# A decoder step on one core: weight forms of the first MLP pair earlier, squares loaded by another queue, last weights kept

## The chip, the core and the metric

The kernel runs on one core of a Trainium2 chip. The core has five engines with a queue of instructions each: TensorE (PE in the profile) multiplies, VectorE (DVE) and ScalarE (ACT) work element by element, GpSimd (POOL) does a little of that and issues DMAs, SyncE (SP) only issues DMAs. Each engine takes its instructions in order; semaphores order the engines among each other. SBUF is the memory that the engines work from, PSUM the memory that TensorE writes to, and DRAM is reached by DMA.

The metric is the time of one execution on the device, in microseconds (us), and of several runs the median.

## What is computed

One layer of a decoder for a prompt of 1024 tokens and 8 samples of 8 tokens, 1088 columns in all, width 1024, all in float32. Four token mixers share one input projection; their outputs are projected, gated, summed and projected again. Then comes the part that the change touches:

```python
x = x + g1 * out                                        # out = (gated sum of the branches) @ w_out
h2 = rmsnorm(x, p["norm_mlp_g"][l]) * (1.0 + sc2) + sh2
x = x + g2 * (jnp.square(jax.nn.relu(h2 @ p["w_mlp1"][l])) @ p["w_mlp2"][l])
...
y = rmsnorm(x, p["norm_final_g"])
```

w_mlp1 is 1024 x 4096, w_mlp2 4096 x 1024.

## The kernel before

**Layout and products.** Activations lie with the features on 128 partitions and the 1088 columns along the free axis: eight tiles for the width, 32 for the hidden layer. A float32 product is made of three products of a rounded format: each operand is split into a high part (a rounded copy, ACT) and a low part (what is left, DVE), by `split`, and hi x hi, lo x hi and hi x lo are summed in PSUM. A weight block of 512 x 128 is loaded to a staging tile `wst` by SP's queue and split to `whi` and `wlo` (`weights`). There are three buffers of `wst` and four each of `whi` and `wlo`, so a load waits for a split, and a split for the products that read the old block.

**Order.** Nothing is ordered by hand here: a scheduler orders every engine's instructions by a priority (program order, unless `tc.high_priority(offset=...)` moves a piece ahead by that many instructions) and by a simulated clock. Weight blocks and evacuations of PSUM are moved ahead by `PRIO` = 3000 instructions, the second half's column forms by twice that. The order is fixed when the program is built, and an engine whose next instruction has to wait holds everything behind it.

**Memory.** Pools of SBUF are stacks, one from the left and one from the right end. A pool that is closed gives its place to later pools, and a tile there waits until the instructions that used the overlapping old tiles are done.

**w_out and the columns' forms.** The 1088 columns are two halves (`HALF` = 544) of two quarters (`QU` = 272). For each half, `w_out` is multiplied from the tiles M, the residual is added (`add_resid`) and the squares are summed for the norm (`add_sq`). `norm_terms(c)` and `column_forms(c)` then make, for half c, the norm's factor and seven operands called B11, B21, T1 to T4 and B22: parts of the normalised half and differences of such parts. `column_forms(0)` runs beside the second half's w_out; `column_forms(1)` needs w_out's last sums.

**MLP1** is a product of 2 x 2 blocks made with seven block products instead of eight. `seven_weights` loads the four blocks of two row tiles (a11, a12, a21, a22), makes four sums and differences of them on DVE (s3, s1, s2 and the last one, in place but for s3, which has the tile `wcm`) and splits seven forms, W1 to W7. They are made in the order W1, W2, W5, W6, W7, W4, W3. The first four lie in the pool `wp` that all weights use, the last three in a pool `xw`, which also holds a22 and `wcm`. `xw` is the last pool on the left, above the forms, where w_out's operands M were. `seven` multiplies the forms: pa, pb, pe, pc are its PSUM tiles, each with W1, W2, W5 or W4 first, and W6, W7, W3 added later. There are 16 such pairs of row tiles, `j`; for the first one `seven` runs once for each half, later for both halves at once. Each of the 14 products of a pair is 12 TensorE products. `evac` squares the result, splits it and stores the two parts to DRAM (`asc`, tensors ah and al) by POOL's queue.

**MLP2** takes the 32 hidden tiles in groups (`GROUPS`). The first two stay in SBUF (`KK`); all others are loaded again, as two tiles of 544 KB each, into `NA` = 9 buffers for each part, by SP's queue. For each group and each of the eight row tiles `mt`, `gemm_quarters` multiplies the group's blocks of w2 with the columns and `ev` adds to the residual R. In the second group the residual from before the MLP is loaded (`xr`) and added. The last group runs over three column groups, (0, 1), (2,) and (3,), so that the final norm of one can run beside the next. It loads and splits its eight w2 blocks in each of them. After each column group come the norm's product over the partitions (`rms`), Ln and Exp on ACT, and the multiplication, by ACT and POOL for the first two and part of the last, by DVE for the rest.

## Time and profile before

| | us |
|---|---|
| median of 3 runs | 2477.72 |
| lowest and highest of them | 2475.24, 2478.2 |
| the profiled execution | 2474.55 |
| its span, first to last instruction | 2472.8 |
| TensorE busy within the span | 2394.4 |
| VectorE, ScalarE, GpSimd busy | 1375.8, 1035.5, 306.0 |

The profile is one execution. A page gives each engine's busy time, 40 slices of the span, DMA queues, and the chain of work that ended last. A row of time order reads: start, length, engine, line, operation, output<-inputs, shape, count, and in brackets how long the engine had stood idle and what ended that. A line like L107 is that of a helper (`mm`), so tile names tell more than lines. A row of windows reads: from and to, length, busy time and count, granted TensorE clock (1.00 is full), DMA share, GB/s. The stages that matter here lie so in the span: w_out to 1694 us, MLP1 from there to about 2055, MLP2 to the end.

### The profile page before, as it was taken

To read this page: it belongs to the slowest core of one execution; us is meant where nothing else is said; L and a number is where in the kernel's file an instruction comes from. 1 tells how busy PE (TensorE), PEld (TensorE's weight loads), DVE (VectorE), ACT (ScalarE), POOL (GpSimd) and SP (SyncE) were. 2 spreads that over 40 slices of the span, in tenths; PEclk is the share of its full clock that TensorE was granted. 3 is DMA by queue.
4 is the path that set the end of the run, shared out by engine and by line. 5 is a ranking of instruction groups with operands and counts; after the bars stand their busy time and mean duration, and the time that the engine had idled before them with its cause. 6 is when DMAs were issued, how large, how long until landed. Compare 5 with 4: busy or idle time off the path is not lost.

```text
span 2472.8 us, 46690 instructions
## 1 busy us (share of the span) xinstructions
PE 2394.4 (97%) x19150; PEld 2236.7 (90%) x19150; DVE 1375.8 (56%) x2540; ACT 1035.5 (42%) x1849; POOL 306.0 (12%) x479
## 2 busy tenths in 40 slices
PE   6999999999999999999999999997999999999996
PEld 4998898988998988889888999997999998999996
DVE  6666445746266473656734676768655552422247
ACT  5522545225344234542256553455666663111115
POOL 0102200012101021000111000001222221000003
PEclk9999999999999999999999999999999999999998
DMA  7333221241322232213322464532655657425244
GB/s 258 129 88 95 94 70 63 80 111 57 106 69 70 81 94 91 74 64 85 100 90 107 148 215 164 175 120 89 184 155 154 158 151 266 156 100 189 68 153 135
DMA packets 189140, 300.45 MB, mean 122 GB/s; under 512 B 57320, under 2 KB 105400, under 8 KB 188928
## 3 DMA queue, kind: packets, MB, share of 16 engines
q1 hardware_dynamic: 138512, 217.79, 27.9%
q0 software_dynamic: 47104, 74.44, 9.9%
q10 hardware_dynamic: 3312, 5.25, 0.6%
q8 instruction: 150, 2.46, 0.4%
q14 instruction: 62, 0.51, 0.1%
HBM read 211.29 MB, written 81.66 MB: 118 GB/s over the span
## 4 chain that ended last, share of the span: by engine, by line
PE 83%; DVE 7%; DMA 4%; ACT 3%; issue 2%; SPq 0%; ACTq 0%; DVEq 0%; POOL 0%; POOLq 0%
PE pg L107 57%; PE pa L107 6%; PE pe L107 4%; PE sm L107 2%; PE pc L107 2%; PE pb L107 2%; PE pu L107 2%; DVE X L101 2%; PE ada L107 1%; PE G L107 1%; PE pyr L107 1%; PE po L107 1%; DMA adaw<-ada 1%; DVE wlo L101 1%; DMA g<-gst 1%
## 5 line engine op out<-in xcount | busy, mean ns | idle before, releaser
L107 PE MATMUL pg<-Hh,whi 128*128 128x362 f32 (+1 forms) x1872 | 625.9, 335 | 1.0 <-ACT gst L98 0.7
L107 PE MATMUL pg<-Hh,wlo 128*128 128x362 f32 (+1 forms) x1872 | 626.6, 335 | 0.0
L107 PE MATMUL pg<-Hl,whi 128*128 128x362 f32 (+1 forms) x1872 | 621.0, 334 | 0.0
L98 ACT ACTIVATE whi<-wst 128x512 fp32r<-128x512 f32 (+1 forms) x404 | 250.0, 620 | 609.7 <-PE pg L107 534.8
L101 DVE TENSOR_TENSOR wlo<-wst,whi 128x512 fp32r<-128x512 f32 (+1 forms) x404 | 278.5, 690 | 380.9 <-ACT whi L98 380.1
L107 PEld LDWEIGHTS pg<-Hh,whi 128*128 128x128 f32 x1872 | 352.6, 188 | 12.5 <-issue 2.3
L107 PEld LDWEIGHTS pg<-Hl,whi 128*128 128x128 f32 x1872 | 352.3, 189 | 8.5 <-DVE Hl L104 0.8
L107 PEld LDWEIGHTS pg<-Hh,wlo 128*128 128x128 f32 x1872 | 352.9, 189 | 7.6
L107 PE MATMUL pg<-ah,whi 128*128 128x272 f32 x960 | 276.4, 290 | 2.9 <-ACT whi L98 2.9
L107 PE MATMUL pg<-ah,wlo 128*128 128x272 f32 x960 | 277.3, 290 | 1.4 <-DVE wlo L101 1.4
L107 PE MATMUL pg<-al,whi 128*128 128x272 f32 x960 | 273.8, 290 | 0.0
L107 PEld LDWEIGHTS pg<-ah,whi 128*128 128x128 f32 x960 | 181.9, 190 | 3.5 <-ACT whi L98 3.3
L107 PEld LDWEIGHTS pg<-ah,wlo 128*128 128x128 f32 x960 | 182.1, 190 | 2.2 <-DVE wlo L101 2.0
L107 PEld LDWEIGHTS pg<-al,whi 128*128 128x128 f32 x960 | 180.3, 190 | 0.0
L104 DVE SCALAR_TENSOR_TENSOR cacc<-u,pv,cacc 128x1024 f32<-128x1024 f32 x120 | 153.8, 1281 | 2.1
L104 DVE SCALAR_TENSOR_TENSOR R<-pg,mod,R 128x544 f32<-128x544 f32 (+2 forms) x120 | 65.7, 570 | 136.7 <-PE pg L107 136.7
L107 PE MATMUL pg<-yh,whi 128*128 128x362 f32 (+1 forms) x384 | 127.5, 332 | 1.1 <-DVE gt L101 1.1
L107 PE MATMUL pg<-yh,wlo 128*128 128x362 f32 (+1 forms) x384 | 126.6, 330 | 0.0
L107 PE MATMUL pg<-yl,whi 128*128 128x362 f32 (+1 forms) x384 | 126.2, 329 | 0.0
L1181 POOL DMA_DIRECT2D g<-gst x96 | 53.5, 557 | 390.0 <-ACT gst L98 377.5
L98 ACT ACTIVATE gst<-pg 128x362 f32<-128x362 f32 (+1 forms) x96 | 45.4, 473 | 126.2 <-PE pg L107 111.6
L699 POOL TENSOR_SCALAR sp<-St,dec 128x64 f32<-128x64 f32 x60 | 58.5, 975 | 229.2 <-DVE St L104 208.0
(443 smaller groups left out, 4757.3 us busy)
## 6 DMA issues: line engine op xcount, KB each, us to landing
wst<-w SPq DMA_DIRECT2D x136, 256.0 KB, 3.3
adaw<-ada SPq DMA_DIRECT2D x48, 512.0 KB, 7.2
wst<-w_in SPq DMA_DIRECT2D x92, 256.0 KB, 2.9
gt<-g SPq DMA_DIRECT2D x32, 544.0 KB, 4.1
wst<-w_gate SPq DMA_DIRECT2D x64, 256.0 KB, 2.9
ah<-ah POOLq DMA_DIRECT2D x60, 272.0 KB, 2.7
al<-al POOLq DMA_DIRECT2D x60, 272.0 KB, 4.3
ah<-ah SPq DMA_DIRECT2D x30, 544.0 KB, 9.0
```

The source lines that it names most:

```text
L98: return self.nc.scalar.activation(out, in_, func, bias=bias, scale=scale)
L101: return self.nc.vector.tensor_tensor(out, a, b, op=op)
L104: return self.nc.vector.scalar_tensor_tensor(out, a, s, b, op0=op0, op1=op1)
L107: return self.nc.tensor.matmul(out, lhsT, rhs, start=start, stop=stop, skip_group_check=True)
L699: nc.gpsimd.tensor_scalar(sp, St, dec[:, c:c + 1], None, op0=OP.mult)
L1181: nc.gpsimd.dma_start(d[:, n0:n0 + n], t[:, :n])
```

## The change

It has these parts.

- **First pair's weight forms.** The pool `xw` is on the right now, between the two residual pools, and open before w_out. `seven_weights` for the first pair (`W0`) stands right behind `column_forms(0)` in the program, ahead of `column_forms(1)`. Of the seven forms, the first two and the last two lie in `wp` and the middle three in `xw`.
- **Column forms.** Each form is one tile of four blocks instead of four tiles. `column_forms` works on four blocks with one operation in the first half and on two in the second. The tile `sqt` in w_out is a quarter wide instead of a half.
- **MLP2's loads.** They go by GpSimd's queue. The groups are (0, 1), (2, 3), (4..11), (12..19), (20..27), (28..31); before they were (0, 1), (2..7), (8..15), (16..23), (24..27), (28..31). The loaded tiles lie lowest in their memory, the residual above them; `xr` and `sqt` have a pool of their own.
- **Last group.** Its eight split blocks are kept in a pool `fw` and used for all three column groups. The final norm of a column group stands behind the third row tile of the next one. Its multiplications are done by DVE, except k = 2 and 5 of the last column group, which ACT and POOL do as before.

```diff
-    def weights(self, ap, prio=True):
+    def weights(self, ap, prio=True, pool=None, bufs=WHI):
...
-            hi = self.wp.tile([128, 4, 128], F32R, name="whi", tag="whi", bufs=WHI)
-            lo = self.wp.tile([128, 4, 128], F32R, name="wlo", tag="wlo", bufs=WHI)
+            hi = (pool or self.wp).tile([128, 4, 128], F32R, name="whi", tag="whi", bufs=bufs)
+            lo = (pool or self.wp).tile([128, 4, 128], F32R, name="wlo", tag="wlo", bufs=bufs)
...
-        for j, (ap, ks) in enumerate(parts):
-            hi, lo = self.weights(ap)
+        for j, (W, ks) in enumerate(parts):
+            hi, lo = W if isinstance(W, tuple) else self.weights(W)
...
-                pool = self.wp if next(n) < 4 else self.xw
+                pool = self.wp if next(n) in (0, 1, 5, 6) else self.xw
...
-    pools = right(last, "resb"), right(ractx, "resa")
+    xctx = ExitStack()
+    pools = [right(last, "resb")]
+    net.xw = right(xctx, "xw")
+    pools.append(right(ractx, "resa"))
...
-        part = lambda k, h: R[:, k, h * QU:h * QU + QU]
+
+        step = 2 if c else 4
+        part = lambda k, h: R[:, k:k + step, h * QU:h * QU + QU]
+
+        def split_form(f, i, src):
+            net.split(F[f][0][c][:, i:i + step], F[f][1][c][:, i:i + step], src)
+
         for f, o in (("B11", 0), ("B21", 4)):
-            for i in range(4):
-                normed(i + o)
+            for i in range(0, 4, step):
+                for k in range(i, i + step):
+                    normed(k + o)
                 split_form(f, i, part(i + o, 0))
...
-            for i in range(4):
+            for i in range(0, 4, step):
                 net.tt(part(i + out[0], out[1]), part(i + a[0], a[1]), part(i + b[0], b[1]), OP.subtract)
                 split_form(f, i, part(i + out[0], out[1]))
-        for i in range(4):
+        for i in range(0, 4, step):
             split_form("B22", i, part(i + 4, 1))
...
-                F[f][p][c] = [fpool.tile([128, QU], F32R, name=f"{f}{'hl'[p]}{c}{i}") for i in range(4)]
-    net.xw = left(fctx, "xw")
+                F[f][p][c] = fpool.tile([128, 4, QU], F32R, name=f"{f}{'hl'[p]}{c}")
     column_forms(0)
+    W0 = net.seven_weights((A["w1"][0], A["w1"][1]))
     net.stage.close()
...
-                W = net.seven_weights((A["w1"][2 * j], A["w1"][2 * j + 1]))
+                W = net.seven_weights((A["w1"][2 * j], A["w1"][2 * j + 1])) if j else W0
...
-            rp, ap_ = left(m, "resid"), left(m, "ap")
+            ap_, rp, mp = left(m, "ap"), left(m, "resid"), left(m, "misc")
...
-            GROUPS = ((0, 1), (2, 3, 4, 5, 6, 7), tuple(range(8, 16)), tuple(range(16, 24)), (24, 25, 26, 27), (28, 29, 30, 31))
+            GROUPS = ((0, 1), (2, 3)) + tuple(tuple(range(i, i + 8)) for i in (4, 12, 20)) + ((28, 29, 30, 31),)
...
-                            nc.sync.dma_start(x.bitcast(F32), d[k].bitcast(F32))
+                            nc.gpsimd.dma_start(x.bitcast(F32), d[k].bitcast(F32))
...
+                def last_norm(qs):
+                    sl = slice(qs[0] * QU, qs[-1] * QU + QU)
                     ps = net.pqt("rms")
-                    for i, q in enumerate(cs[0]):
+                    for i, q in enumerate(qs):
...
                     for k in range(KB8):
                         r, t = R[k][:, sl], rstd[:, sl]
-                        if cs[0] != (3,) or k % 3 == 2:
+                        if qs == (3,) and k % 3 == 2:
                             net.act(r, r, AF.Copy, scale=net.p("norm_final_g", k))
                             nc.gpsimd.tensor_tensor(r, r, t, op=OP.mult)
                         else:
                             net.stt(r, r, net.p("norm_final_g", k), t, OP.mult, OP.mult)
                         (nc.sync if k % 2 else nc.scalar).dma_start(A["y"][k][:, sl], r)
-    last.close()
+
+                columns = ((0, 1), (2,), (3,)) if final else (((0, 1), (2, 3)),)
+                if final:
+                    last.close()
+                    fw, kept = right(m, "fw"), []
+                for n, qs in enumerate(columns):
+                    for mt in range(8):
+                        if not final:
+                            net.gemm_quarters(parts(ks, mt), Y, ev, qs)
+                        else:
+                            if n == 0:
+                                kept.append(net.weights(A["w2"][ks[0] // 4, mt], pool=fw, bufs=8))
+                            net.gemm_quarters([(kept[mt], ks)], Y, ev, (qs,))
+                        if gi == 1:
+                            x = mp.tile([128, NT], F32, name="xr", tag="xr", bufs=1)
...
+                        if final and n and mt == 2:
+                            last_norm(columns[n - 1])
+                if final:
+                    last_norm(columns[-1])
```

More of the change, by code (lines that the diff above doesn't have):

```diff
@@ L32 @@
 GN_EPS = 64e-5
+PRIO = 3000
+WST, WHI = 3, 4
 LN_EPS = 1e-5
@@ L255, in product @@
             for i in range(4):
[L256 to L258 removed]
+                self.mm(ps[:, c, :QU], hi[:, i, :], xh[c][:, i], start=start and i == 0, stop=False)
+                self.mm(ps[:, c, :QU], lo[:, i, :], xh[c][:, i], start=False, stop=False)
+                self.mm(ps[:, c, :QU], hi[:, i, :], xl[c][:, i], start=False, stop=i == 3)
     def pqt(self, name):
@@ L1267, in add_resid, with add_sq @@
                 net.tt(r[:, e:n], r[:, e:n], t.rearrange("p s t -> p (s t)"), OP.add)
-    def add_sq(acc, r, mt, pool):
-        t = pool.tile([128, HALF], F32, name="sqt", tag="sqt", bufs=2)[:, :r.shape[-1]] if mt else None
+    def add_sq(acc, r, mt, pool, width):
+        t = pool.tile([128, width], F32, name="sqt", tag="sqt", bufs=2)[:, :r.shape[-1]] if mt else None
         net.sumsq(acc, r, t)
@@ L1292, in normed @@
             net.act(r[:, :e], r[:, :e], AF.Identity, bias=net.modp(3, k))
-        def split_form(f, i, src):
-            net.split(F[f][0][c][i], F[f][1][c][i], src)
         if c:
@@ L1332, in ev @@
                     add_resid(r, half * HALF + n0, ps[:, :n], n, mt, 2)
-                    add_sq(accs[:, n0:n0 + n], r, mt, ops[half])
+                    add_sq(accs[:, n0:n0 + n], r, mt, ops[half], QU)
                 net.gemm(A["w_out"][mt], KB8, (lambda k: M[half][0][k], lambda k: M[half][1][k]), ev, HALVES[0])
@@ L1434, in ev @@
                         sl = slice(qs[0] * QU, qs[-1] * QU + QU)
-                        add_sq(accs[:, sl], r[:, sl], mt, ap_)
-                for cs in (((0, 1),), ((2,),), ((3,),)) if final else (((0, 1), (2, 3)),):
-                    for mt in range(8):
-                        net.gemm_quarters(parts(ks, mt), Y, ev, cs)
-                        if gi == 1:
-                            x = ap_.tile([128, NT], F32, name="xr", tag="xr", bufs=1)
-                            for h in range(2):
-                                nc.sync.dma_start(x[:, h * HALF:h * HALF + HALF], xsp[h][:, mt, :])
-                            net.tt(R[mt], R[mt], x, OP.add)
-                    if not final:
-                        continue
-                    ps = net.pqt("rms")
-                    for i, q in enumerate(cs[0]):
-                        sl = slice(q * QU, q * QU + QU)
-                        net.mm(ps[:, i, :QU], net.ones, accs[:, sl])
-                        net.lnp(rstd[:, sl], ps[:, i, :QU], 1.0 / D, net.eps)
-                        net.exph(rstd[:, sl])
-                    sl = slice(cs[0][0] * QU, cs[0][-1] * QU + QU)
+                        add_sq(accs[:, sl], r[:, sl], mt, mp, HALF)
+                def last_norm(qs):
+                    sl = slice(qs[0] * QU, qs[-1] * QU + QU)
+                    ps = net.pqt("rms")
+                    for i, q in enumerate(qs):
+                        s = slice(q * QU, q * QU + QU)
+                        net.mm(ps[:, i, :QU], net.ones, accs[:, s])
+                        net.lnp(rstd[:, s], ps[:, i, :QU], 1.0 / D, net.eps)
+                        net.exph(rstd[:, s])
                     for k in range(KB8):
                         r, t = R[k][:, sl], rstd[:, sl]
-                        if cs[0] != (3,) or k % 3 == 2:
+                        if qs == (3,) and k % 3 == 2:
                             net.act(r, r, AF.Copy, scale=net.p("norm_final_g", k))
@@ L1462, in trunk_kernel @@
                         (nc.sync if k % 2 else nc.scalar).dma_start(A["y"][k][:, sl], r)
-    last.close()
+                columns = ((0, 1), (2,), (3,)) if final else (((0, 1), (2, 3)),)
[12 more added lines that the diff above has]
+                            x = mp.tile([128, NT], F32, name="xr", tag="xr", bufs=1)
+                            for h in range(2):
+                                nc.sync.dma_start(x[:, h * HALF:h * HALF + HALF], xsp[h][:, mt, :])
+                            net.tt(R[mt], R[mt], x, OP.add)
+                        if final and n and mt == 2:
+                            last_norm(columns[n - 1])
+                if final:
+                    last_norm(columns[-1])
 def _pack(i):
```

6 lines of the change are left out of this document (1 added, 5 removed).

## The prediction

> **What bounds the kernel now.** I read the page's 40 slices first (each digit the busy tenths of one). Then I laid windows over the places where the slices dip and asked there for TensorE's waits, by whom each was ended.
>
> ```profile
> PE   6999999999999999999999999997999999999996
> 1741.35 3.03 PE pe L107 x24
> 1650.00:1694.09 44.09, 40.51 (x315) 1.00 0.33 111
> 1694.09:1731.12 37.03, 24.30 (x141) 0.87 0.25 73
> 2049.90:2100.00 50.10, 44.47 (x332) 0.97 0.83 290
> 2100.00:2422.80 322.80, 322.80 (x2574) 1.00 0.38 132
> 2422.80:2472.80 50.00, 29.09 (x203) 0.82 0.46 146
> ```
>
> The slices show TensorE (PE) busy nearly everywhere, with dips at the start, after two thirds and at the end; so an edit can win only where PE stands still or runs slowly. The row of the chain in order of time (1741.35) gives the full pace: 24 products in 3.03 us, 0.126 us each. The window rows (length, PE busy and count, granted clock, DMA share, GB/s) then give the loss of a stage as its length less its products at that pace. **Start of MLP1:** 37.03 - 141 x 0.126 = 19.2 us. **From MLP1 to MLP2:** 50.10 - 332 x 0.126 = 8.3. **Last column groups:** 2 x 8 x 12 = 192 products, 24.2 us, so 25.8 of 50.0. Between, from 2100 to 2422.8, nothing is lost. The change works in just these three places; what w_out loses before 1694 (44.09 - 315 x 0.126 = 4.4) it touches on the way.
>
> **Start of MLP1.** Below: the two waits of PE in 1694 to 1731 that end with a weight form (us in all, times, longest), one load on SP's queue, two windows of DVE (its busy time and count in place of PE's), DVE's operations that read the staged weights in 1694 to 1731.5 (ns least, median, most), and three single rows of DVE.
>
> ```profile
> PE pe L107 <- ACT whi L98: 2.5, 1, 2.5
> PE pe L107 <- DVE wlo L101: 2.5, 1, 2.5
> 1695.23 0.33 SPq L226 DMA_DIRECT2D wst<-w  x1
> 1676.00:1694.00 18.00, 12.43 (x34) 1.00 0.36 122
> 1694.00:1731.50 37.50, 35.75 (x82) 0.87 0.25 72
> L101 DVE TENSOR_TENSOR wlo<-wst,whi x8: 684/686/693, 1698.8 to 1731.4; 128x512 fp32r<-128x512 f32 x8
> L101 DVE TENSOR_TENSOR wst<-wst x6: 683/684/693, 1698.1 to 1729.8; 128x512 f32<-128x512 f32 x6
> L101 DVE TENSOR_TENSOR wcm<-wst x2: 685/686/686, 1695.1 to 1717.6; 128x512 f32<-128x512 f32 x2
> 1708.41 1.49 DVE L101 TENSOR_TENSOR B11l<-rh,B11h 128x272 fp32r<-128x272 f32 x4
> ...
> 1730.36 1.14 DVE L101 TENSOR_TENSOR T4l<-rh,T4h 128x272 fp32r<-128x272 f32 x3
> 2029.66 0.72 DVE L101 TENSOR_TENSOR x<-pe,u 128x544 f32<-128x544 f32 x1 [2.58 <-ACT u L98]
> ```
>
> The fourth weight block of the first pair has its tile in xw, whose memory lies on that of w_out's operands, so its load is issued only at 1695.23, after w_out's last product. Every sum and form behind it (W5, then W6, W3, W4) is late, and PE waits 2.5 + 2.5 for W5. But DVE is full: 35.75 of 37.50 us. The last form of the second half, T4l, begins at 1730.36, and PE runs at full pace only from 1731.12. **The path here is DVE's sum of work up to T4l, not the weights alone.**
>
> With xw on the right and `W0` made before `column_forms(1)`, nine DVE operations of the first pair (five low parts, four sums) can leave this window. At 0.69 us less the overlap of neighbours, some 0.61 each, that is 5.5 us. DVE has 18.00 - 12.43 = 5.6 idle us in 1676 to 1694 to take them in, and column_forms(0) in four-wide operations frees more. But a form in wp needs a buffer that w_out's last products release, so I count seven of nine: 4.3. Merging two column operations into one saves little: two of four neighbours cost 2 x 0.35 ((1.49 - 0.44) / 3), a 544-wide one 0.64 with the same overlap taken off, so 22 x 0.06 = 1.3. The waits of ACT behind the late load give about 0.5; DVE evacuates the first half within the same time, 0.4 against. Sum 5.7 of the 19.2. The rest stays, since the second half's forms cannot begin before w_out's last evacuation. Bounds: all nine, the merge and all 1.75 idle us of DVE, 8.5; below, minus 3: the moved operations sit ahead of a w_out evacuation on DVE, which is what a 2.77 us wait at 1667.87 shows already, and would make a second such wait. Taken: 5.7, nearest to what DVE's rows add up to.
>
> ```profile
> 1667.87 0.36 PE L107 MATMUL pg<-Mh,whi 128*128 128x272 f32 x1 [2.77 <-DVE t L101]
> ```
>
> The loads of `W0` pass no queue that anyone waits on: SP gives them out after w_out's last weights, by order and because those hold the wst buffers first.
>
> **From MLP1 to MLP2.** PE's waits in 2049.9 to 2100, then queues: SP's loads of the squares (KB each, median us from issue to landing; 2055 to 2082), POOL's issues from 1700 on, and DVE's operations in 2100 to 2157.
>
> ```profile
> PE pg L107 <- ACT whi L98: 2.9, 2, 1.7
> PE pg L107 <- ACT R L98: 1.4, 1, 1.4
> PE pg L107 <- DVE wlo L101: 1.4, 2, 1.2
> ah<-ah SPq DMA_DIRECT2D x9, 544.0 KB, 9.7
> al<-al SPq DMA_DIRECT2D x9, 544.0 KB, 14.1
> L1372 POOL DMA_DIRECT2D al<-al x68 | 49.6, 812 | 45.8 <-DVE al L101 38.7 <-DVE R L101 4.0 <-DVE wlo L101 2.8
> L1372 POOL DMA_DIRECT2D ah<-ah x68 | 45.4, 693 | 238.4 <-ACT ah L98 238.4
> L101 DVE TENSOR_TENSOR R<-R,xr 128x1088 f32<-128x1088 f32 x6 | 7.8, 1292 | 0.2
> L104 DVE SCALAR_TENSOR_TENSOR R<-pg,mod,R 128x544 f32<-128x544 f32 x7 | 5.5, 785 | 13.5 <-PE pg L107 13.5
> ```
>
> Eighteen loads of the squares stand in SP's queue, and weight loads stand behind them; PE waits 5.7 us for weights and one evacuation, and the other 2.6 of the 8.3 are slow products after the waits. After the change group (2, 3) needs two pairs of squares where (2..7) needed six, its 24.2 us of products (8 x 24 x 0.126) cover the other seven pairs, and no weight stands behind a square. The weight waits (2.9 + 1.4) and the slow products go. What may stay is the 1.4: ACT waits there for stores of the last squares, which now share POOL's queue with the loads. New: in group (2, 3) DVE has per row tile the evacuation (0.79 for the first half, as much for the second in two pieces, small ones for the sample columns: about 1.9), 0.4 of a half-wide low part and 1.29 of the added residual, 3.6 against 3.03 of PE. The sums can run late into the next group, so 1.4 us rather than 8 x 0.6 = 4.8. Taken: 8.3 - 2.8 = 5.5; bounds 0 and 8.3.
>
> What the loads cost on POOL: 60 issues in 400 us at 0.7 to 0.8 us each, on an engine that has nothing else before the last group; a pair takes 1.5 us to issue, and at 16 x 0.8 = 13 us a group of eight stays far below the 97 us that it lasts. The three boundaries at which eight tiles give way are the tight spots, since nine buffers leave one spare; before, there were two of them and no product waited there (the row 2100 to 2422.8). I cost them at nothing; that hangs on POOL's loads streaming as SP's do.
>
> The Trainium skill ("SBUF — State Buffer", section "SBUF: two separate sides") speaks against this move: a DMA from GpSimd's queue needs descriptors that GpSimd writes, and it cannot write them while certain DVE operations hold the port that both share. By that rule POOL's issues would stretch beside DVE. The rows above (0.69 and 0.81 us beside a busy DVE in MLP1) show no such stretch, so I give it only the chance of the last rival below.
>
> **The last columns.** PE's rows around its two stops and its last product, POOL's and DVE's beside them, all by start, and a 544-wide group of DVE from 1643 to 1694 for its price.
>
> ```profile
> 2425.49 0.70 PE L107 MATMUL rms<-accs,ones 128*128 128x272 f32 x2 [2.42 <-DVE accs L101]
> 2431.48 12.88 POOL L1459 TENSOR_TENSOR R<-R,rstd 128x544 f32<-128x544 f32 x8 [361.59 <-ACT rstd L98]
> 2433.32 1.58 DVE L101 TENSOR_TENSOR accs<-accs,sqt 128x272 f32<-128x272 f32 x1
> ...
> 2446.55 0.43 DVE L101 TENSOR_TENSOR accs<-accs,sqt 128x272 f32<-128x272 f32 x1
> 2447.03 1.28 PE L107 MATMUL rms<-accs,ones 128*128 128x272 f32 x2 [8.22 <-DVE accs L101]
> ...
> 2461.55 0.28 PE L107 MATMUL pg<-al,whi 128*128 128x272 f32 x1
> L104 DVE SCALAR_TENSOR_TENSOR rh<-rh,mod,rstd 128x544 f32<-128x544 f32 x8 | 5.7, 777 | 0.1
> ```
>
> PE stops twice, 2.42 and 8.22 us, because the norm's product stands in its order right behind a column group and needs DVE's last sum. DVE is late since it splits the same eight blocks again for each column, and while POOL multiplies (from 2431.48, 12.88 us) one sum takes 1.58 us instead of 0.43. The change keeps the split weights, puts the norm three row tiles into the next column, and moves its multiplications for the first two column groups to DVE. Then in column 2 DVE has per tile 0.41 (a residual), 0.35 (a sum of squares, 0.43 alone) and 0.71 (5.7 / 8), 1.47 us against 1.51 of PE; in column 3, with the sample columns' small operations and 272-wide multiplications, some 1.6 against 1.51, so it ends about 0.5 late. The stage becomes 24.2 of products, six norm products at 0.35, 2.1, the same 11.0 from PE's last product (2461.83) to the end, and 0.5: 37.8 instead of 50.0. **12.2 us.** Late next is DVE in column 3. Bounds: 9 (DVE each tile as late as its 544-wide operations may make it, some 0.2 x 16) and 14 (the tail shorter by POOL's and the stores' share).
>
> **Sum:** 5.7 + 5.5 + 12.2 = 23.4. The profiled execution took 2474.55 us (span 2472.8), so 2451.1 by its own time; the median of the three runs, 2477.72, stands 3.2 above it and would give 2454.3. I forecast 2453.
>
> **Rivals.**
> - *The second half's column path takes it all:* the first pair's operations are replaced on DVE by the second pair's, and T4l comes no earlier. For it: DVE's 95% in that window, where of 17 weight operations (16 in the rows, one low part of wcm) eight are the second pair's. Against: those wait for buffers that PE frees. Then 17.7 remain: 2459.
> - *The border keeps its loss:* 18 loads still fill the DMA engines in the same 25 us and group (2, 3) is paced by DVE. The Trainium skill ("DMA: Bandwidth & Descriptors", section "Issuing engines are not separate DMA queues") says that all queues run on the same 16 DMA engines and that another issuer saves only issue time; the trace has the DMA engines at 0.83 from 2049.9 to 2100, by whichever queue. Against: two pairs are enough for the first 24 us. Then 17.9 remain: 2459.
> - *More than forecast:* w_out's 4.4 shrinks by its 2.77 too, and all three stages reach their upper bounds: 8.5 + 8.3 + 14 + 2.8 = 33.6, 2443.
> - *POOL's loads land one after another,* so that PE stalls at the boundaries into (12..19), (20..27) and (28..31). The old tiles come free only in the last row tile of a group, the first four some 7.6 us before its end (its second weight block, 48 products, and the last quarter of the first, 12), and the next group's first products need the spare and three new pairs. With a time p for a pair the stall is 3p - 7.6 each. If a load waits for the one before it, p is two times the 4.3 us that a store of half the size takes to land in the row below: 18.2 us of stall, three times, 2453 + 55 = 2508, slower. It decides from 3p - 7.6 = 23.4 / 3 = 7.8 on, p = 5.1; between 4.5 and 5.6 nothing measurable is left either way. For it: no load on POOL stands in the trace. Against: POOL issues its stores at 0.7 to 0.8 us each, several within one landing time.
>
> ```profile
> ah<-ah POOLq DMA_DIRECT2D x60, 272.0 KB, 2.7
> al<-al POOLq DMA_DIRECT2D x60, 272.0 KB, 4.3
> ```
>
> **How the numbers follow.** Forecast 0.56, column path 0.14, border 0.12, more than forecast 0.07: all faster, 0.89. POOL's pair time from 4.5 to 5.6, no change, 0.05 (within 0.2%, some 5 us, about what a measurement of this kernel can tell from none); longer, slower, 0.06. The range takes in the first four with their bounds: 2441 to 2466.
>
> **What would show it.** Right: in the changed profile the pair's fourth block is loaded before 1690 and no `pe` product waits for whi or wlo near 1700; T4l ends near 1725; PE's longest wait from 2050 to 2100 is under 1.5 us; the norm product waits under 1 us; 38 us, not 50, lie between the last group's first column group and the end. Wrong: waits of `pg` for ah or al behind a boundary, POOL issues far over 0.8 us, T4l still some 36 us after w_out, or new waits before 1694.

## The result

The changed kernel takes 2459.73 us (median of 4 runs, 2457.73 to 2460.25) against 2476.48 for the kernel before on the same chip (4 runs), a ratio of 0.9929 with a 95% interval of 0.9917 to 0.9941: 16.8 us faster. The forecast was 2453, the range 2441 to 2466. The sign and the range held, and so did the three places. What each part of the change does there came out otherwise, and most of this text is about that.

The profiled execution took 2457.73 us, with a span of 2456.0. First the 40 slices of the changed kernel's page, then windows over the same stretches as before, counted from the same events (length, TensorE busy and its count, granted clock, DMA share, GB/s).

```profile
PE   6999999999999999999999999998999999999997
```

```profile
1651.50:1695.60 44.10, 40.94 (x319) 0.99 0.38 129
1695.60:1728.50 32.90, 22.69 (x142) 0.81 0.22 61
2047.90:2098.00 50.10, 50.10 (x402) 1.00 0.82 287
2098.00:2414.00 316.00, 315.35 (x2504) 1.00 0.37 132
2414.00:2456.00 42.00, 27.13 (x203) 0.88 0.30 107
```

The dip after two thirds is shallower (8 and no 7) and the one at the end smaller. Loss is length less products at 0.126 us, as in the prediction:

- **End of w_out:** 44.10 - 319 x 0.126 = 3.9, from 4.4.
- **Start of MLP1:** 32.90 - 142 x 0.126 = 15.0, from 19.2: 4.2 gained, where 5.7 was forecast.
- **From MLP1 to MLP2:** 402 products in 50.10 us, no loss left of 8.3. But from the last MLP1 product to the end of the last group's first column group it is 367.2 us before and 360.4 after, a gain of 6.8: some 2 us went elsewhere in MLP2.
- **Last column groups:** 42.0 us instead of 50.0: 8.0, where 12.2 was forecast.

0.5 + 4.2 + 6.8 + 8.0 is 19.5, and the span shrank by 16.8. Of the difference 0.6 is in the rest of MLP1 (1728.5 to 2047.9, 319.4 us; before, 1731.12 to 2049.9, 318.8). The rest lies ahead of these stages: the profile of after reaches w_out's first product with the low part of M (`pg<-Ml`, 1.1 us behind w_out's very first) 2.0 us later (1594.4 against 1592.4), with as many instructions of each engine ahead of it. In the other profiles below this landmark lies anywhere from 1592.7 to 1605.5, also in kernels whose part ahead of w_out is that of before. It is scatter between executions, and it goes with the granted clock of the whole execution: the six runs of the changed kernel when it was run again (after_again below) go from 2456.0 us at a clock of 0.993 to 2471.08 at 0.988, the slower ones at the lower clocks. Single profiles are therefore compared here by stage and not by their ends.

TensorE's waits in 1694 to 1731 (us in all, times, longest), its rows at the end of the last group, by start, and the last norm product of before:

```profile
PE pa L109 <- DVE T2l L103: 2.9, 1, 2.9
PE rms L109 <- DVE accs L103: 2.7, 1, 2.7
PE pe L109 <- DVE T1l L103: 2.6, 2, 2.3
PE pa L109 <- ACT T2h L100: 2.5, 1, 2.5
PE pa L109 <- DVE B11l L103: 2.0, 1, 2.0
```

```profile
2433.43 0.73 PE L109 MATMUL rms<-accs,ones 128*128 128x272 f32 x2 [1.00 <-DVE accs L103]
...
2441.27 0.29 PE L109 MATMUL pg<-al,whi 128*128 128x272 f32 x1
2445.21 0.94 PE L109 MATMUL rms<-accs,ones 128*128 128x272 f32 x2 [3.65 <-DVE accs L103]
```

```profile
2464.22 0.70 PE L107 MATMUL rms<-accs,ones 128*128 128x272 f32 x2 [2.39 <-DVE accs L101]
```

No product of the first pair waits for a weight form now (before: 2.5 + 2.5 for W5). In their place stands a wait of 2.7 for w_out's last sum of squares (`accs`), and the waits for the second half's column forms are still there. The wait of 2.77 in w_out that the prediction shows (1667.87) is gone too; "The start of MLP1" below comes back to it. In the last group, of the stops of 2.42 and 8.22 us one is gone and the other is 1.00, but the last one has grown from 2.39 to 3.65.

### The profile page after: what moved, and what is told of

Same layout as the page of the kernel before. It is cut to its first block, busy times and chain, and to the rows that moved or that the text cites. A ratio compares the mean times of both kernels' runs of the same rounds, so it can differ in the third digit from the quotient of the medians.

```text
span 2456.0 us, 46456 instructions
## 1 busy us (share of the span) xinstructions
PE 2392.7 (97%) x19150; PEld 2235.1 (91%) x19150; DVE 1358.9 (55%) x2485; ACT 1008.6 (41%) x1782; POOL 318.4 (13%) x523
## 4 chain that ended last, share of the span: by engine, by line
PE 74%; issue 10%; DVE 7%; DMA 5%; ACT 3%; POOL 1%; ACTq 0%; DVEq 0%; POOLq 0%
PE pg L109 47%; PE pa L109 6%; PE pe L109 3%; PE sm L109 2%; DVE X L103 2%; PE pc L109 2%; PE pb L109 2%; PE pu L109 2%; PE ada L109 1%; DMA al<-al 1%; PE G L109 1%; PE pyr L109 1%; PE po L109 1%; DMA ah<-ah 1%; DVE wlo L103 1%
## 5 line engine op out<-in xcount | busy, mean ns | idle before, releaser
L103 DVE TENSOR_TENSOR wlo<-wst,whi 128x512 fp32r<-128x512 f32 (+1 forms) x388 | 261.9, 676 | 430.3 <-ACT whi L100 429.4
L100 ACT ACTIVATE whi<-wst 128x512 fp32r<-128x512 f32 (+1 forms) x388 | 239.6, 619 | 597.8 <-PE pg L109 493.7
```

Source lines behind the costliest of these rows:

```text
L100: return self.nc.scalar.activation(out, in_, func, bias=bias, scale=scale)
L103: return self.nc.vector.tensor_tensor(out, a, b, op=op)
```

## The experiments

Twelve more runs, one of them the changed kernel again; none leaves out any part of the computation. Each ratio is to the kernel before on the same chip (medians of 2479.54, 2478.45 and 2479.26 us for the three batches); it is taken from the runs and not from the two medians, so it can differ from their quotient in the last digits. The stages come from one profile each and are right to 0.1 us: from the landmark at w_out's start (`pg<-Ml`) to the last product of MLP1; from there to the last product; from there to the end. All count from the start of a product.

| kernel | median us | ratio [95%] | w_out + MLP1 | MLP2 | tail |
|---|---|---|---|---|---|
| before | | 1 | 463.2 | 405.9 | 11.3 |
| after | 2459.73 | 0.9929 [0.9917, 0.9941] | 459.2 | 387.7 | 14.7 |
| a_only | 2469.88 | 0.9967 [0.9953, 0.9980] | 459.6 | 398.5 | 11.3 |
| b_only | 2476.54 | 0.9987 [0.9978, 0.9996] | 464.2 | 402.6 | 12.7 |
| c_only | 2468.16 | 0.9955 [0.9943, 0.9967] | 464.5 | 392.3 | 12.3 |
| c_ysync | 2460.90 | 0.9926 [0.9912, 0.9939] | 463.2 | 387.3 | 14.4 |
| a_c | 2455.49 | 0.9915 [0.9901, 0.9928] | 459.9 | 385.8 | 12.9 |
| b_sp | 2467.09 | 0.9950 [0.9938, 0.9962] | 459.8 | 395.2 | 12.8 |
| c_cols | 2461.68 | 0.9923 [0.9908, 0.9937] | 459.8 | 387.0 | 12.8 |
| xw_right | 2470.58 | 0.9968 [0.9958, 0.9978] | 464.0 | 398.4 | 11.5 |
| a_c_cols | 2452.22 | 0.9900 [0.9883, 0.9917] | 459.9 | 385.6 | 11.0 |
| after_again | 2460.36 | 0.9929 [0.9910, 0.9948] | 462.1 | 387.3 | 14.4 |
| a_late | 2463.84 | 0.9933 [0.9916, 0.9950] | 461.6 | 387.3 | 14.4 |
| a_step1 | 2465.78 | 0.9947 [0.9933, 0.9961] | 465.0 | 387.1 | 15.0 |

### The three parts alone

**a_only** is the kernel before with the first pair's part: xw on the right, W0 early, wide column forms.

```diff
+    net.xw = right(xctx, "xw")
...
+    W0 = net.seven_weights((A["w1"][0], A["w1"][1]))
...
-            for i in range(4):
+            for i in range(0, 4, step):
```

> Before plus the first-pair part alone (pool xw on the right, W0 early, wide column forms). Theory, the three places are independent: from the first B11 product to the last product of MLP1 358.0 us as in the changed kernel (361.5 before), the rest as before, so 3.5 to 4 us faster, 0.15%. The forecast's own sum was 5.7. Rival, the scheduler's order of MLP1 depends on what follows and the place gains nothing alone: 361 to 362 us, no change.

**b_only** is the kernel before with MLP2's loads on GpSimd's queue, the new groups and the new order in memory.

```diff
-                            nc.sync.dma_start(x.bitcast(F32), d[k].bitcast(F32))
+                            nc.gpsimd.dma_start(x.bitcast(F32), d[k].bitcast(F32))
...
-            GROUPS = ((0, 1), (2, 3, 4, 5, 6, 7), tuple(range(8, 16)), tuple(range(16, 24)), (24, 25, 26, 27), (28, 29, 30, 31))
+            GROUPS = ((0, 1), (2, 3)) + tuple(tuple(range(i, i + 8)) for i in (4, 12, 20)) + ((28, 29, 30, 31),)
```

> Before plus the border alone (squares by GpSimd's queue, groups (2, 3) and (4..11) to (20..27), loaded tiles lowest in memory). Theory, independent: no wait of pg between 2045 and 2100 and 6 to 7 us faster, 0.27%, as the landmarks of the changed kernel say (367.2 us from the last MLP1 product to the end of the last group's first column group before, 360.4 after). Rival, the gain at the border comes out of an earlier end of MLP1 and not out of this part: 2 to 3 us.

**c_only** is the kernel before with the last group's weights kept, and its norm later and on DVE.

```diff
+                            if n == 0:
+                                kept.append(net.weights(A["w2"][ks[0] // 4, mt], pool=fw, bufs=8))
+                            net.gemm_quarters([(kept[mt], ks)], Y, ev, (qs,))
...
+                        if final and n and mt == 2:
+                            last_norm(columns[n - 1])
```

> Before plus the last group alone (weights kept, norm three row tiles later, multiplications on DVE). Theory, independent: the last product comes 27.5 us after the first column group (39.0 before), the tail behind it grows from 11.0 to 14.4 us, 8 us faster in all, 0.33%. Rival, the longer tail in the changed kernel comes from the other parts (stores or loads still under way): tail 11 to 11.5 and 11 to 12 us faster.

By their ratios the parts alone gain 0.33, 0.13 and 0.45 per cent, 0.91 together, where the whole change gains 0.71. The intervals are too wide to call that an overlap, but the stages show one: in MLP2 the three gain 7.4, 3.3 and 13.6 us, 24.3 together, and the whole change 18.2. By the medians b_only gains 3.0 us and not 6 to 7, since its tail is 1.4 longer than that of before. c_only gains 11.4 and not 8: its tail is 12.3, nearer to the 11.3 of before than to the 14.7 of the change, as its rival had it. And a_only, which touches nothing behind MLP1, gains 9.7 and not 3.5 to 4, most of it in MLP2 (405.9 to 398.5). Here are SP's issues around the end of MLP1, of before (MLP1's last product starts at 2055.6) and of a_only (2052.8); in a row with x5 the duration runs from the first issue to the last.

```profile
2042.24 12.37 SPq L159 DMA_DIRECT2D wst<-w  x3
2054.72 0.37 SPq L1422 DMA_DIRECT2D ah<-ah  x1
...
2061.27 0.32 SPq L1422 DMA_DIRECT2D al<-al  x1
2064.04 0.33 SPq L159 DMA_DIRECT2D wst<-w  x1
```

```profile
2044.95 16.11 SPq L159 DMA_DIRECT2D wst<-w  x5
2061.16 0.39 SPq L1430 DMA_DIRECT2D ah<-ah  x1
...
2063.73 0.33 SPq L159 DMA_DIRECT2D wst<-w  x1
```

Before, ten loads of the squares are issued one behind the other from 2054.72 on, and the next weight block stands behind them at 2064.04. In a_only five weight blocks go first; the squares begin 8.4 us after MLP1's last product instead of 0.9 before it, and a weight block comes after every four of them. The window behind MLP1 in a_only shows what that does (columns as above):

```profile
2052.80:2092.80 40.00, 40.00 (x322) 1.00 0.98 352
```

The DMA engines are busier (0.98) than before in the same 40 us (0.94), and TensorE does not wait at all. The loss at this border was never the amount of transfers; it was weight blocks standing behind squares in one queue.

**xw_right** is the kernel before with xw's place alone (and the narrower `sqt` that this needs).

```diff
-    pools = right(last, "resb"), right(ractx, "resa")
+    pools = [right(last, "resb")]
+    net.xw = right(xctx, "xw")
+    pools.append(right(ractx, "resa"))
```

> Before with only the pool xw moved to the right (and the scratch of squares in w_out a quarter wide for its room); W0 in its old place, column forms, border and last group as before. Theory, the place of xw clears the border: from the last MLP1 product to the end of the first column group 358 to 360 us (367.2 before), and the fourth block of the first pair is loaded before 1690; 7 to 9 us faster. Rival, the early W0 does it through the order of the instructions: the border stays at 366 to 367 and the kernel is at most 2 us faster.

MLP2 takes 398.4, as in a_only: xw's place does all of it, by way of the order in which the scheduler puts SP's issues (five weight blocks ahead of the squares here too). Why it orders them so is not in a trace. And w_out with MLP1 takes 464.0: the first pair's weights, now no longer held back by w_out's operands, bring nothing there on balance. More on that below.

### The border part beside the others

**a_c** is the changed kernel with the border part undone: loads by SP, old groups, old order in memory.

```diff
-                            nc.gpsimd.dma_start(x.bitcast(F32), d[k].bitcast(F32))
+                            nc.sync.dma_start(x.bitcast(F32), d[k].bitcast(F32))
...
-            GROUPS = ((0, 1), (2, 3)) + tuple(tuple(range(i, i + 8)) for i in (4, 12, 20)) + ((28, 29, 30, 31),)
+            GROUPS = ((0, 1), (2, 3, 4, 5, 6, 7), tuple(range(8, 16)), tuple(range(16, 24)), (24, 25, 26, 27), (28, 29, 30, 31))
```

> The changed kernel with the border's part undone (loads of squares by SP again, the old groups and memory order), first-pair part and last group kept. Theory: with xw on the right the border has nothing left to lose, as the run of the first-pair part alone shows (358.4 us from the last MLP1 product to the end of the first column group; 360.4 in the changed kernel), and the end behind the last store is 2.3 us shorter without loads on GpSimd's queue; so 3 to 4 us faster than the changed kernel. Rival: the border's part is needed beside the other two, and the kernel is 4 to 7 us slower than the changed one.

**b_sp** is the changed kernel with the loads by SP, the new groups and order in memory kept.

```diff
-                            nc.gpsimd.dma_start(x.bitcast(F32), d[k].bitcast(F32))
+                            nc.sync.dma_start(x.bitcast(F32), d[k].bitcast(F32))
```

> The changed kernel with only the queue undone: squares loaded by SP, new groups and memory order kept. Theory, the queue brings nothing and costs the end: from the last landing of y to the end of the span 1.3 us as before instead of 3.5, no wait of pg between 2045 and 2110, 1 to 3 us faster. Rival, the queue carries the border: PE waits again for whi behind the squares, 3 to 6 us slower.

a_c is not slower than the change; its stages are shorter, 1.9 us in MLP2 and 1.8 in the tail, and its ratio is lower (0.9915 to 0.9929, with overlapping intervals). b_sp loses 7.5 us in MLP2 (395.2 against 387.7), and one wait of TensorE names the cause:

```profile
PE pg L109 <- ACT whi L100: 4.0, 1, 4.0
```

With the new groups and SP's queue only two weight blocks go ahead of the squares, and not five. The one that TensorE waits for is issued at 2074.57 behind fourteen squares, and ACT can split it only at 2085.29; what else is lost is slow products behind this wait. So the new groups need GpSimd's queue; the old groups, with xw on the right, need neither.

Where do the 1.9 us of MLP2 go? Windows of 40 us over MLP2, first of the change, then of a_c:

```profile
2133.60:2173.60 40.00, 40.00 (x321) 1.00 0.22 64
2173.60:2213.60 40.00, 39.74 (x315) 1.00 0.68 259
...
2293.60:2333.60 40.00, 39.61 (x313) 1.00 0.56 215
```

```profile
2172.90:2212.90 40.00, 40.00 (x321) 1.00 0.15 47
...
2332.90:2372.90 40.00, 40.00 (x321) 1.00 0.73 268
```

321 products go into 40 us. The change loses 6 and 8 of them in two windows, 14 x 0.126 = 1.8 us, both where the loads of the next eight pairs run (DMA share 0.68 and 0.56) and the group changes. a_c loses none, although its transfers are as dense (0.73). Nor does b_sp, which has the new groups: all its windows of 40 us from 2137.4 to 2417.4 have 321 products. From 2125 to 2400 TensorE's only waits in the change are two for a load of the squares, and b_sp has none; this wait, and b_sp's two windows in which most loads run:

```profile
PE pg L109 <- DMA ah<-ah: 0.5, 2, 0.3
```

```profile
2177.40:2217.40 40.00, 40.00 (x321) 1.00 0.48 178
...
2297.40:2337.40 40.00, 40.00 (x321) 1.00 0.69 263
```

So the queue costs this, and not the groups. The other five kernels with these loads and groups and xw on the right lose 1.1 to 1.4 us there. The loads themselves: POOL's issues of `ah` in the change (busy us, mean ns), their size and median time from issue to landing (KB, us), and the same of b_sp, which differs from the change in nothing but the queue:

```profile
L1430 POOL DMA_DIRECT2D ah<-ah x30 | 16.6, 554 | 279.9 <-PE pg L109 269.3 <-DMA ah<-ah 7.5 <-DMA al<-al 2.8
ah<-ah POOLq DMA_DIRECT2D x30, 544.0 KB, 10.5
```

```profile
ah<-ah SPq DMA_DIRECT2D x30, 544.0 KB, 7.5
```

Issuing is cheap, 0.55 us, and nothing stretches it. But the loads land later. The two medians show that too large: the trace has a landing for all 30 loads of the change and for only seven of the 30 by SP's queue. At the same place in a group, the fifth, seventh and twelfth load of (12..19) and (20..27), a load takes 8.1, 9.9, 12.5 and 8.2, 11.3, 12.6 us to land in the change and 7.5, 8.8, 11.4 and 7.4, 9.2, 11.0 in b_sp: 0.6 to 2.1 us more from GpSimd's queue. Why it does, no run shows.

### The end of the kernel

**c_ysync** is the changed kernel with all stores of y by SP, to see whether ACT's stores delay the last squares.

```diff
-                        (nc.sync if k % 2 else nc.scalar).dma_start(A["y"][k][:, sl], r)
+                        nc.sync.dma_start(A["y"][k][:, sl], r)
```

> The changed kernel with all stores of y issued by SP and none by ACT. Theory: the tail of 14.4 us comes from ACT's queue, where four store issues wait for DVE's multiplications of column 2 and hold the squares of column 3 behind them (4.03 us idle before one square); without them the tail goes to 11 to 12 us and the kernel is 2 to 3 us faster than the changed one. Rival: DVE's own queue, where eight multiplications stand ahead of evacuations, sets the tail: 14 us as before and no change.

**c_cols** is the changed kernel with the last group's columns in the order (2, 3), (1,), (0,), so that the sample columns' small operations fall into the first column group.

```diff
-                        if qs == (3,) and k % 3 == 2:
+                        if qs == (0,) and k % 3 == 2:
...
-                columns = ((0, 1), (2,), (3,)) if final else (((0, 1), (2, 3)),)
+                columns = ((2, 3), (1,), (0,)) if final else (((0, 1), (2, 3)),)
```

> The changed kernel with the column groups of the last group in the order (2, 3), (1,), (0,), so that the columns of the samples, with three more DVE operations in each row tile, come first. Theory, DVE's queue makes the tail: per row tile of the last column group it has 0.76 us less the samples' 0.42, the wait of the norm product of 3.65 us shrinks to 1 or 2 and the tail of 14.4 to 12 us; 2 to 3 us faster. Rival, the tail is latency from engine to engine: 14 us, no change.

In c_ysync the last norm product waits 3.65 us as before, so ACT's stores are not it. In c_cols it waits less:

```profile
2449.80 0.73 PE L109 MATMUL rms<-accs,ones 128*128 128x272 f32 x2 [2.04 <-DVE accs L103]
```

So it is DVE's own queue in the last column group. DVE of the change, there:

```profile
2437.10 2.15 DVE L106 SCALAR_TENSOR_TENSOR R<-R,pv,rstd 128x272 f32<-128x272 f32 x5
...
2440.47 0.21 DVE L103 TENSOR_TENSOR t<-pg,mod 128x64 f32<-128x64 f32 x1
...
2444.07 0.99 DVE L103 TENSOR_TENSOR accs<-accs,sqt 128x272 f32<-128x272 f32 x2
```

Five multiplications of the column group before stand ahead of the last tiles' residuals, and then each tile needs several operations for its sample columns. TensorE's last product is at 2441.27; DVE ends its sums at 2445.06. The tail of c_cols is 1.8 us shorter (12.86 against 14.68); in the ratio (0.9923, interval overlapping the change's) so little can't be seen.

The other piece of the longer tail stands in the chain of waits. Its last step is DVE's last multiplications, in the change, b_only, a_c_cols and c_only:

```profile
2448.58 2.15 DVE R L106 x4
```

```profile
2465.72 1.65 DVE R L104 x4
```

```profile
2444.47 2.15 DVE R L106 x4
```

```profile
2460.45 2.15 DVE R L106 x4
```

From the end of these to the end of the span it is 2456.0 - 2450.73 = 5.3 us in the change, 2472.2 - 2467.37 = 4.8 in b_only, 2450.0 - 2446.62 = 3.4 in a_c_cols and 2465.7 - 2462.6 = 3.1 in c_only. So it is in all fourteen profiles: 4.8 to 5.3 in the seven kernels that load the squares by GpSimd's queue, 3.1 to 3.4 in the seven that load them by SP's. b_sp (3.1) against the change is this one edit. Some 2 us at the end belong to the loads' queue, although the last load is long done. They are spent in GpSimd's DRAIN, the closing instruction of its program. Its rows (x3: shortest, median and longest in ns; first and last start), in the change and in b_sp:

```profile
L1572 POOLq DRAIN  x3: 40/93/7996, 2447.2 to 2455.7; - x3
```

```profile
L1572 POOLq DRAIN  x3: 40/93/2932, 2458.8 to 2465.0; - x3
```

In the change the long one ends at 2455.17, 1.8 us after SyncE is through with its own waits for the stores (2453.38), and the last steps of all engines come only behind it. In the seven kernels with loads on GpSimd's queue it ends 6.0 us after GpSimd's last operation, in the other seven 1.1 us after it, although those too store by this queue up to the end of MLP1. What it waits for, the trace does not show.

**a_c_cols** puts together what these runs favour: the change with the border part undone (as in a_c) and the column order of c_cols.

> The change with its border part undone (the squares' loads, groups and memory order of before), and the last group's column groups in the order (2, 3), (1,), (0,), so that the sample columns' small operations fall into the first column group and not into the last. Nothing of the computation is left out. Theory: the border part is redundant once xw is on the right and lengthens the end, and DVE in the last column group sets the last norm's wait; the two effects add: the last norm product waits about 2.0 us instead of 3.65, from the last product to the end about 11.3 us (12.9 without the new order, 14.5 in the change), MLP1's end to the last product about 386; 1.6 to 2 us less than with the old order (0.9915), so a ratio near 0.991 and about 5 us below the changed kernel. Rival: the wait only moves to another place, the end of the span stays as it was; then 0.9915 and 12.9 us.

The norm product waits 2.04 us, the tail is 11.0, MLP2 385.6: the two gains add. 2452.22 us is 8.1 below the changed kernel on the same chip (**after_again**, the changed kernel itself). The stages account for 5.1 of them, 1.7 in MLP2 and 3.4 in the tail; most of the rest is ahead of MLP2 (462.1 against 459.9 in these profiles), where the two kernels have the same instructions. The intervals of the two ratios still overlap a little (0.9917 and 0.9910), so the order of the two is likely and their distance not settled.

> The changed kernel itself, so that the others stand beside it on one chip. Theory (variation between executions explains the 1.6 us that its first profile lost before 55 us): ratio 0.993; first w_out product to first product of MLP1 plus MLP1 near 459 us; the last norm product waits 3.65 us again and the end follows 10.2 to 10.8 us behind that product's start. Rival: the late start belongs to the kernel; then the first product of the w_out stage is again about 2 us later than in the profile of before.

### The start of MLP1

after_again confirms the ratio. But its w_out with MLP1 took 462.1 us and not 459.2, and the wait for `accs` was 4.9 us and not 2.7. Here is DVE's first operation on the first pair's weights, in the first profile of the change and then in after_again:

```profile
1685.64 0.69 DVE L103 TENSOR_TENSOR wcm<-wst 128x512 f32<-128x512 f32 x1 [0.38 <-DMA wst<-w]
```

```profile
1698.85 0.69 DVE L103 TENSOR_TENSOR wcm<-wst 128x512 f32<-128x512 f32 x1 [2.57 <-DMA wst<-w]
```

From the landmark it is 91.2 us in the one and 93.4 in the other: a load that lands 2.2 us later, with w_out's last sums queued behind the operation that waits for it. c_ysync has the same (93.2), which explains 2 of the 4 us that its 463.2 lies above the first profile; the other 2 are in MLP1 and stay unexplained.

**a_late** is the change with the first pair's forms written in the loop again, behind the second half's column forms.

```diff
-    W0 = net.seven_weights((A["w1"][0], A["w1"][1]))
...
-                W = net.seven_weights((A["w1"][2 * j], A["w1"][2 * j + 1])) if j else W0
+                W = net.seven_weights((A["w1"][2 * j], A["w1"][2 * j + 1]))
```

> The change, but the first pair's seven weight forms are made in the loop again, behind the second half's column forms in the program. Nothing of the computation is left out. Theory: the early forms bring the 4.0 us before and in MLP1's start (the run with xw alone on the right gained nothing there): first w_out product to MLP1's end is back at 463 to 464 us, the products of the first pair wait for whi or wlo near 1695 again, and the rest is as in the change, so 4 us slower than it (ratio about 0.9945). Rival: the wide column forms bring the 4 us: it stays at 459 to 460 us and 0.993.

**a_step1** is the change with column forms made block by block.

```diff
-        step = 2 if c else 4
+        step = 1
```

> The change, but the column forms are made block by block as before (56 subtractions and splits of one block per half instead of 14 of four and 28 of two); the first pair's weight forms stay early. Nothing of the computation is left out. Theory: with DVE full to the last column form, what the merging saves is only the fixed part of each operation, about 1 us: first w_out product to MLP1's end 460 to 461 us. Rival: the merging brings most of the 4.0 us: 463 to 464 us.

Both theories fell. a_late has no weight wait, and all its instructions stand on every engine in the order of the change, so moving the statement does nothing: a_late is the change once more, and its 461.6 is another sample of the scatter. Weight forms are 3000 instructions ahead by priority in either place, and only memory held them back before. And a_step1 is slow: 465.0 us in w_out with MLP1, as slow as before, and 5.4 us above the change on the same chip by the medians (the intervals overlap). So, with the weight forms early, the wide column forms bring what is gained here. xw_right says the same from the other side, 464.0 with the forms early and the columns narrow.

The early forms by themselves only move time: in these two kernels the way from the landmark to MLP1's first product is 104.6 and 103.9 us, where it is 101.7 to 102.1 in the three with late ones, and MLP1 from its first product to its last is 360.4 and 360.1 us, where it is 361.6 to 362.4. No kernel here has wide column forms and late weight forms, so what the wide ones would bring alone is open. In all, the five profiles with narrow forms lie at 463.2 to 465.0, whether the weight forms are early or not; the nine with wide ones at 459.2 to 463.2, six of them below 460.

Where the wide forms gain it, TensorE's waits in w_out show first: one row of a_step1, then all waits of the change from 1596 to 1694.

```profile
1672.62 0.36 PE L109 MATMUL pg<-Mh,whi 128*128 128x272 f32 x1 [2.76 <-DVE t L103]
```

```profile
PE pg L109 <- DVE t L103: 0.5, 2, 0.3
```

`t` is a piece of an evacuation, and column forms and weights' low parts stand ahead of it on DVE. All five narrow profiles have this wait, 2.75 to 2.77 us long and 75.5 us behind the landmark; it is the one at 1667.87 in the prediction. None of the nine wide ones has it. Their last w_out product starts 97.5 us behind the landmark, and that of the narrow ones at 100.7 to 101.1. What follows is seen in SP's issues of the first pair's weights and in DVE's first operation on them, in xw_right (landmark at 1594.8), a_step1 (1597.1) and the change (1594.4; its DVE row stands above):

```profile
1681.54 17.96 SPq L226 DMA_DIRECT2D wst<-w  x7
1689.42 0.69 DVE L101 TENSOR_TENSOR wcm<-wst 128x512 f32<-128x512 f32 x1 [3.15 <-DMA wst<-w]
```

```profile
1683.81 18.13 SPq L228 DMA_DIRECT2D wst<-w  x7
1691.92 0.69 DVE L103 TENSOR_TENSOR wcm<-wst 128x512 f32<-128x512 f32 x1 [3.37 <-DMA wst<-w]
```

```profile
1677.52 17.38 SPq L228 DMA_DIRECT2D wst<-w  x7
```

With narrow forms the first of these loads is issued 86.7 us after the landmark, with wide ones 83.1; DVE's operation comes at 94.6 and 94.8 against 91.2. The first half's forms run on DVE beside w_out. With 11 subtractions and low parts instead of 44 there (22 in the second half; the 56, 14 and 28 of the expectation are high and low parts, without the subtractions), DVE comes to the evacuation in time. All that follows is then earlier: SP issues the first pair's loads 3.6 us earlier, and w_out's last sums, behind them on DVE, come earlier too. From the landmark to MLP1's first product it is 101.2 us and not 103.9 or 104.6. The rest, 0 to 2 us, is in MLP1.

## Why the prediction was right, and where it was wrong

**Start of MLP1, 5.7 forecast, 4.2 in the first profile; over the nine profiles with this part 0 to 4.0 in w_out and MLP1 together, the median 3.3.** The mechanism was taken wrongly; that the size came near is luck, since two errors offset each other.

- "I count seven of nine: 4.3." The operations did leave the window, yet a gain does not follow: xw_right and a_step1 have the early forms and stand at 464.0 and 465.0, where the kernels with the old start have 463.2 to 464.5. What decides is in the prediction only as its lower bound, "the moved operations sit ahead of a w_out evacuation on DVE": that wait is there, 2.7 us, 4.9 where the load lands late. Not DVE's sum of work up to T4l was the path but a chain through the load, DVE's first sum and w_out's last sums. One of the prediction's own signs of being wrong shows it, "T4l still some 36 us after w_out": its last row starts 35.6 us after w_out's last product has ended (37.7 before).
- "w_out's 4.4 shrinks by its 2.77 too" stands only in the rival that gains more, at 0.07 for all of it. This piece came true in all nine wide profiles, and the new wait for `accs` takes most of it back: the end of w_out shows 0.5.
- "Merging two column operations into one saves little", 22 x 0.06 = 1.3. The rate was right: 55 operations fewer save 3.8 us of DVE's busy time between a_step1 and a_late (1363.4 and 1359.6), 0.07 each. The count left out the 33 of the first half, which the text mentions ("frees more") and does not cost. The runs give merging some 4 to 5 us (464.0 and 465.0 less the 459.9 that is the median of the nine), since it also moves the loads.
- "The loads of `W0` pass no queue that anyone waits on" held for SP. It missed that w_out's sums on DVE wait behind the operation that needs such a load.

**From MLP1 to MLP2, 5.5 forecast, 6.8 measured.** The first-pair part alone would have given 8.8 (a_only: 358.4 us to the end of the first column group, from 367.2), the border part alone 5.0 (b_only: 362.2). The prediction ascribed the gain to the border part, whose size it got, and gave xw's move no effect here; xw_right shows that effect. The expected leftover of 1.4 and late sums in group (2, 3) did not appear: 402 products in 50.10 us.

**"I cost them at nothing"**, of POOL's loads, was wrong by some 3 to 4 us: 1.1 to 1.8 at the group changes, 2 at the end. The rival that the loads land one after another is refuted in its size (it needed over 7.8 us of stall at each of three boundaries; the two that show lost 0.8 and 1.0) but right in its place. The Trainium skill ("SBUF — State Buffer", section "SBUF: two separate sides") says that descriptor writing on GpSimd is held up while certain DVE operations hold a shared port. The issues at 0.55 us beside a working DVE show none of that, and whether the later landings have to do with it is open. Its other rule ("DMA: Bandwidth & Descriptors", section "Issuing engines are not separate DMA queues"), that all queues share the same DMA engines, agrees with their share in the 40 us behind MLP1, 0.94 with the squares on SP's queue (before) and 0.94 with them on GpSimd's (the change). The rival drawn from it, that the border keeps its loss, does not follow: the order within the issuing queue decided.

**Last columns, 12.2 forecast, 8.0 measured.** The columns themselves went from 39.0 to 27.5 us, forecast 26.3 (24.2 + 2.1). "The same 11.0 from PE's last product" (from its end) "to the end", with 0.5 added, is the step that failed: it was 14.4. Of the 3.4 more, 2 are the loads' queue, by way of GpSimd's DRAIN, which the prediction did not connect with the end. 1.3 are the last norm's wait, 3.65 from 2.39: "late next is DVE in column 3" was right, and 0.5 too small. With both taken away, a_c_cols needs 38.3 us from the first column group to the end, where the prediction had 37.8.

## What to carry to other kernels

Before an edit is credited with removing a wait, find out what stands ahead of the waiting instruction in its queue, and try each part of a merged change alone: here one pool's place did the work that a new queue and new groups were meant for, and the new queue then cost 3 to 4 us by the stages. Moving a statement in a scheduled kernel may change nothing; look whether the order on each engine changed. Count merged operations in every stage that they run in, also where the engine seems to have time, because a load or a buffer may hang on them.

## What the runs showed of the hardware that was not expected

- With the squares' 60 loads on GpSimd's queue, the time from the last arithmetic to the end of the execution is 4.8 to 5.3 us instead of 3.1 to 3.4, in seven profiles against seven, though the last of these loads landed long before. GpSimd's closing DRAIN ends 6.0 us after its last operation, and not 1.1.
- At the same place in a group of loads, a 544 KB load took 0.6 to 2.1 us longer to land from GpSimd's queue than from SP's (8.1 to 12.6 against 7.4 to 11.4 us, six pairs), in kernels that differ in nothing else.
- A 256 KB weight load that the same instructions issue was waited for 2.2 us longer in one execution of the same kernel than in another (93.4 and 91.2 us behind the landmark), and with it a whole stage moved. One profile of one kernel is not enough for an effect of 2 us.
